# The first 34 microseconds of a hybrid decoder step: one norm chain per x tile, a new load order, no low half on GpSimd

## The chip, the cores and the metric

One core of a Trainium2 chip runs the whole program. The metric is the device time of one execution in microseconds; lower is better. The kernel before and after the change compute the same.

## The reference, cut to what matters

The kernel is one inference step of a decoder layer: 1024 prompt rows and 8 sample rows, width 1024. Everything begins with an RMS norm and one wide projection:

```
h = rms_norm(x, ln_g)              # y = x * rsqrt(mean(x*x) + 1e-6) * g, float32
proj = h @ w_in                    # w_in: 1024 x 3480, float32
q_raw, kv_raw, g_raw, z_nsa, u_rw, z_rw, q_mem, z_mem = split_in(proj)
```

The columns feed three groups of heads (sparse attention, an RWKV-7 recurrence, attention into a memory). The recurrence has its 896 columns `u_rw` (from column 1816) mixed with the row before: `u = u_cur + (prev - u_cur) * mu`. The groups are gated, concatenated, projected by `w_out` and added to x. Only the norm and the first 256 of the `u_rw` columns (two blocks of 128) lie in the code that is changed.

## The kernel before, in words

Matmuls keep float32 precision by splitting: each operand is a high part rounded to a shorter format plus a low part (the remainder), and a product is three matmuls: high weight by high h, high weight by low h, low weight by high h. In the profile they are `whi`, `wlo` and `h` (both parts).

The beginning stands in `phase1`. `warm` issues `WARM` matmuls of the identity by itself (tile `p_w`) while the first loads are under way. `load_xs` loads the 8 sample rows, squares them on ScalarE and scales them on VectorE. The SyncE queue loads, in this order: the first block of 128 weight columns (`w_load`, 512 KB, tile `wraw`), the four x tiles of the first half of the prompt (`load_x`, 128 rows and 512 KB each, tile `x`), the second weight block, the four x tiles of the second half. `w_split` makes a block's high half on ScalarE (`whi`, line 273) and its low half on VectorE (`wlo`, line 274), or on GpSimd, as for the second block here. The raw weights have two buffers, and so have the split ones; a third block's load waits until the first block is split, and its split waits until the first block's matmuls are done.

`square_x` squares x tiles on ScalarE with a row sum (`sqx`, line 186). `norm_x` takes two x tiles at a time: `rsqrt` is a chain of small VectorE operations (lines 126 to 137, tiles `rq_a`, `rq_g`, `rq_t`, `rq_r`; 12 of them for two columns, 9 for one column), and then the tiles are scaled in place, three on VectorE (line 197) and one on ScalarE (line 195).

`make_hT` transposes two x tiles (256 prompt rows, a "half" in what follows) on TensorE (tile `p_h`, line 223), eight slices of 128 columns; each slice is then taken out of PSUM as a high part on ScalarE (line 232) and a low part on VectorE (line 233). `make_hTs` does this for the sample rows; their last step, 16 small operations, is GpSimd's (lines 253 and 254), and they are the last 8 of the 520 columns of the tiles `h`. `u_half(0)` makes blocks 0 to 6 of `u_rw`. Blocks 0 and 1 are done in pieces as the halves come: block 0 columns 0 to 256, block 1 the same, then columns 256 to 520 of both. A piece is 24 matmuls (8 slices by 3). `do_u` takes a finished block out of PSUM. From block 2 on a block is 48 matmuls in one go.

The second half of the prompt (`xs1`) is squared after the last high part of the first, normed with the same functions, and transposed between blocks 2 to 6.

The order in which each engine gets its instructions is made at compile time by a list scheduler: it takes instructions in the order in which the code names them, but puts a later one first when the earlier is not ready by its own estimate of times. `tc.issue_after(ins)` ties the instructions of a block of code, on the engine of `ins`, behind it. From the end of this beginning on, TensorE's order is the order of the code (`InOrder`). In front of the engines' queues nothing is reordered: an instruction that waits holds up all that stand behind it on its engine.

Of the kernel before, what the change touches and what calls it, by code (L numbers as in the profile page):

```python
# [19 lines left out]
D = 1024  # L20
T = 1024
NS = 8
# [16 lines left out]
WARM = 34  # L39
# [75 lines left out]
class Step:  # L115
# [65 lines left out]
    def square_x(self, xs):  # L181
        nc = self.nc
        ss = self.small.tile([128, 2], F32, name="ss_x")
        for t, x in enumerate(xs):
            j = self.xp.tile([128, D], BF, name="sqx", tag="sqx", bufs=1)
            self.last_sq = nc.scalar.activation(j[:], x[:], AF.Square, accum_out=ss[:, t:t + 1])
        return ss

    def norm_x(self, xs, t0, ss=None):
        nc = self.nc  # L190
        ss = ss or self.square_x(xs)
        r = self.rsqrt(self.small, ss[:], 2, 1.0 / D, 1e-6)
        for t, x in enumerate(xs):
            if t and t0:
                nc.scalar.activation(x[:], x[:], AF.Copy, scale=r[:, t:t + 1])
            else:
                self.last_x = nc.vector.tensor_scalar(x[:], x[:], r[:, t:t + 1], None, op0=OP.mult)
            self.xn[t0 + t] = x
# [6 lines left out]
    def load_xs(self):  # L205
        nc, I = self.nc, self.I
        x = self.xsn = self.xp.tile([128, D], F32, name="xs", tag="xs")
        nc.scalar.dma_start(x[:NS], I["x_sample"][:, 0, :])
        ss = self.small.tile([128, 1], F32, name="ss_s")
        j = self.xp.tile([128, D], BF, name="sqx", tag="sqx", bufs=1)  # L210
        nc.scalar.activation(j[:NS], x[:NS], AF.Square, accum_out=ss[:NS])
        r = self.rsqrt(self.small, ss[:NS], 1, 1.0 / D, 1e-6, parts=NS)
        nc.vector.tensor_scalar(x[:NS], x[:NS], r, None, op0=OP.mult)

    def make_hT(self, H, half):

        nc = self.nc
        for k0 in range(0, 8, 2):
            pool, tag = (self.pw, "w") if k0 % 4 and H == 0 else (self.ptr, "tr")
            ps = pool.tile([128, 2, 256], F32, name="p_h", tag=tag)  # L220
            for j in range(2):
                for t in range(2):
                    nc.tensor.transpose(ps[:, j, t * 128:(t + 1) * 128],
                                        self.xn[2 * half + t][:, (k0 + j) * 128:(k0 + j + 1) * 128], self.ident[:])
            for j in range(2):
                k = k0 + j
                if len(self.hi[H]) <= k:
                    for x, y in zip((self.hi[H], self.lo[H]), (y[k] for y in self.h8) if H == 0 else self.h_tiles(H, k)):
                        x.append(y)
                g, c = self.v("ln_g", k), slice(half * 256, half * 256 + 256)  # L230
                hi, lo = self.hi[H][k], self.lo[H][k]
                self.last_hi = nc.scalar.activation(hi[:, c], ps[:, j], AF.Copy, scale=g)
                self.last_lo = nc.vector.scalar_tensor_tensor(lo[:, c], ps[:, j], g, hi[:, c].bitcast(F32),  # L233
                                                              op0=OP.mult, op1=OP.subtract)
                yield
# [193 lines left out]
    def phase1(self):  # L429
# [8 lines left out]
        with ExitStack() as ctx:  # L438
# [19 lines left out]
            with ExitStack() as xctx:  # L458
# [4 lines left out]
                self.load_xs()  # L463
                raws = [self.w_load(1816, 128)]
                xs0 = self.load_x(0, range(4))
                raws.append(self.w_load(1816 + 128, 128))
                xs1 = self.load_x(1, range(4))
                self.ready = [self.w_split(raws[0], 128)]
                self.norm_x(xs0[:2], 0)
                scaled = self.last_x.ins  # L470
                self.norm_x(xs0[2:], 2)
                self.ready.append(self.w_split(raws[1], 128, G))
                self.h8 = list(zip(*(self.h_tiles(0, k) for k in range(8))))
                with tc.issue_after(scaled):
                    self.make_hTs()
                first = self.u_half(0)
                with tc.issue_after(self.last_sq.ins):
                    for half in range(2):
                        for _ in self.make_hT(0, half):
                            pass  # L480
                        for _ in range(4):
                            next(first)
                with tc.issue_after(self.last_sq.ins):
                    self.rwkv_open()
                for _ in range(16):
                    next(first)
# [1886 lines left out]
```

## Time and profile before

| | |
|---|---|
| median of 3 runs | 1006.16 us (1002.08 to 1006.5) |
| profiled execution | 1003.45 us |
| its span, first to last instruction | 1001.1 us |
| mean granted TensorE clock | 0.991 |
| TensorE matmuls busy | 948.8 us, 95% |
| VectorE busy | 681.4 us, 68% |
| ScalarE busy | 446.8 us, 45% |
| GpSimd busy | 254.0 us, 25% |

Times in the profile count from the start of the span. PE is TensorE, PEld its loading of weights, DVE VectorE, ACT ScalarE, POOL GpSimd, SP SyncE; a q behind the name is the engine's queue of DMA issues. "L233" is line 233 of the kernel. In a timeline row stand start, length, engine, line, operation, output<-input, shapes and count, and in brackets how long the engine was idle before and what ended that. A row with a count above one merges neighbours. A matmul's length overlaps that of the next, so its rate is read from the starts.

### The profile page before, as it was taken

The numbers are of one execution on the slowest core, as the hardware profiler recorded it, in microseconds if no ns is written. First come the engines' busy times: TensorE is split into PE (matmuls) and PEld (weight loads), VectorE is DVE, ScalarE is ACT, GpSimd is POOL, SyncE is SP. The second block draws the span as 40 slices with busy tenths as digits, with TensorE's granted clock in tenths as the row PEclk, the third lists the DMA queues.
The fourth block names the chain that finished last, engine by engine and source line by source line (L and its number), as shares of the span: only waits on it lengthen the run. The fifth ranks groups of instructions, "written<-read, shape, count | busy, mean of one in ns | idle before, by whom it ended". The sixth has DMA issues, their size and how long they took to land.

```text
span 1001.1 us, 24786 instructions
## 1 busy us (share of the span) xinstructions
PE 948.8 (95%) x9955; PEld 788.9 (79%) x9955; DVE 681.4 (68%) x1954; ACT 446.8 (45%) x1005; POOL 254.0 (25%) x221
## 2 busy tenths in 40 slices
PE   7999999999999998999987999999999988998997
PEld 7998888878887887788865777887878876877874
DVE  6759589756684997633548677676869986357364
ACT  6754224223522432224436656665476665224212
POOL 2000000000000000000008776766578853112010
PEclk9999999999999999999999999999999999999999
DMA  8321313212321162265255223411200064984412
GB/s 283 95 75 40 90 34 117 76 45 74 85 77 34 49 178 67 61 158 135 81 159 171 86 81 116 149 43 45 59 22 16 28 149 130 324 276 160 158 65 76
DMA packets 133978, 104.20 MB, mean 104 GB/s; under 512 B 34593, under 2 KB 121128, under 8 KB 133736
## 3 DMA queue, kind: packets, MB, share of 16 engines
q1 hardware_dynamic: 128904, 90.92, 30.8%
q0 software_dynamic: 3200, 10.49, 3.0%
q8 instruction: 78, 1.28, 0.5%
q10 hardware_dynamic: 1760, 1.21, 0.4%
q14 instruction: 36, 0.29, 0.1%
HBM read 84.00 MB, written 22.78 MB: 107 GB/s over the span
## 4 chain that ended last, share of the span: by engine, by line
PE 65%; DVE 18%; ACT 6%; issue 4%; DMA 3%; POOL 2%; SPq 2%; ACTq 0%; DVEq 0%; POOLq 0%
PE p_pr L87 20%; PE p_pr L284 8%; PE p_out L87 5%; PE p_s L87 4%; PE p_pT L87 4%; PE p_o L87 3%; ACT p L1338 2%; POOL p L1352 2%; PE p_iy L87 2%; DVE nm L1337 1%; PE p_hid L87 1%; PE p_z L87 1%; PE p_it L87 1%; ACT p L1347 1%; DVE pt L1298 1%
## 5 line engine op out<-in xcount | busy, mean ns | idle before, releaser
L1352 POOL TENSOR_SCALAR p<-p,fac 128x640 f32<-128x640 f32 (+7 forms) x128 | 211.5, 1666 | 89.6 <-DVE fac L1349 34.6
L87 PE MATMUL p_pr<-h,whi 128*128 128x512 f32 (+5 forms) x928 | 231.0, 340 | 0.3 <-issue 0.3
L87 PEld LDWEIGHTS p_pr<-h,whi 128*128 128x128 f32 (+1 forms) x928 | 147.3, 184 | 19.0 <-issue 3.0
L87 PE MATMUL p_pr<-h,wlo 128*128 128x512 f32 (+5 forms) x464 | 152.5, 329 | 0.0
L999 POOL MEMSET w2d<- 128x128 f32 x1 | 0.2, 205 | 399.8 <-PE p_yy L87 399.8
L87 PEld LDWEIGHTS p_pr<-h,wlo 128*128 128x128 f32 (+1 forms) x464 | 85.1, 183 | 9.7
L284 PE MATMUL p_pr<-h,whi 128*128 128x256 f32 (+2 forms) x416 | 88.3, 308 | 0.4 <-DVE h L233 0.4
L87 PE MATMUL p_pT<-ident,p 128*128 128x128 f32 x528 | 72.8, 280 | 7.0 <-POOL p L1352 3.5
L87 PE MATMUL p_s<-kh,qs 128*128 128x512 f32 (+3 forms) x191 | 71.1, 380 | 1.9 <-ACT p L1338 1.8
L87 PEld LDWEIGHTS p_pT<-ident,p 128*128 128x128 f32 x528 | 56.8, 140 | 19.6 <-issue 7.1
L87 PE MATMUL p_o<-pt,vs 128*64 128x128 f32 x1056 | 70.0, 282 | 1.1 <-DVE c_r L1272 0.7
L1338 ACT ACTIVATE p<-p_s,nm 128x640 f32<-128x640 f32 (+3 forms) x64 | 55.7, 873 | 32.6 <-DVE nm L1337 26.2
L284 PEld LDWEIGHTS p_pr<-h,whi 128*128 128x128 f32 x416 | 67.4, 192 | 3.6 <-DVE h L233 0.6
L1337 DVE TENSOR_REDUCE nm<-p_s 128x1 f32<-128x640 f32 (+3 forms) x64 | 57.6, 918 | 14.9 <-PE p_s L87 14.9
L274 DVE TENSOR_TENSOR wlo<-wraw,whi 128x1024 fp32r<-128x1024 f32 (+1 forms) x34 | 40.7, 1197 | 35.2 <-ACT whi L273 35.1
L87 PEld LDWEIGHTS p_o<-pt,vs 128*64 128x64 f32 x1056 | 59.0, 140 | 6.7 <-issue 2.7
L284 PE MATMUL p_pr<-h,wlo 128*128 128x256 f32 (+2 forms) x208 | 63.3, 306 | 0.0
L87 PE MATMUL p_s<-kl,qs 128*128 128x512 f32 (+3 forms) x192 | 61.7, 338 | 0.0
L273 ACT ACTIVATE whi<-wraw 128x1024 fp32r<-128x1024 f32 (+1 forms) x35 | 36.4, 1039 | 50.9 <-PE p_pr L87 36.8
L1298 DVE COPY pt<-p_pT 128x512 f32<-128x512 f32 (+1 forms) x72 | 47.8, 670 | 16.2 <-PE p_pT L87 15.9
L1296 ACT ACTIVATE pt<-p_pT 128x512 f32<-128x512 f32 (+1 forms) x72 | 42.1, 587 | 27.6 <-PE p_pT L87 27.2
L87 PE MATMUL p_out<-woh,chi 128*128 128x512 f32 x128 | 52.5, 410 | 0.8 <-ACT woh L2194 0.6
(539 smaller groups left out, 2005.2 us busy)
## 6 DMA issues: line engine op xcount, KB each, us to landing
wraw<-in_w_in_dram SPq DMA_DIRECT2D x34, 512.0 KB
pg<-in_c_pool_dram SPq DMA_DIRECT2D x40, 256.0 KB
pg<-in_c_pool_dram SPq DMA_DIRECT2D x48, 128.0 KB
x<-in_x_prompt_dram SPq DMA_DIRECT2D x8, 512.0 KB
z_d<-zt SPq DMA_DIRECT2D x16, 256.0 KB
cat<-z_d SPq DMA_DIRECT2D x8, 512.0 KB
xres<-in_x_prompt_dram POOLq DMA_DIRECT2D x16, 256.0 KB, 3.8
wor<-in_w_out_dram SPq DMA_DIRECT2D x16, 256.0 KB
```

The lines of the kernel that those rows point to most:

```text
L87: self.last = getattr(self.engine, op)(*a, **k)
L273: nc.scalar.activation(hi[:, :, :n], raw[:, :, :n], AF.Copy)
L274: (low or nc.vector).tensor_tensor(lo[:, :, :n], raw[:, :, :n], hi[:, :, :n].bitcast(F32), op=OP.subtract)
L284: self.last_mm = self.pe.matmul(ps[:m, :b - a], w[:, k, :m], h[k][:, a:b], start=(k == 0 and i == 0), stop=(k == 7 and i == 2))
L999: nc.gpsimd.memset(w2d[:], 0.0)
L1296: nc.scalar.activation(pt[:, :n], ps[:, :n], AF.Copy)
L1298: nc.vector.tensor_copy(pt[:, :n], ps[:, :n])
L1337: V.tensor_reduce(nm[:, h, b:b + 1], ps[:, c0:n1], axis=AX.X, op=OP.max, negate=True)
L1338: A.activation(Ps[h, b][:, :n1 - c0], ps[:, c0:n1], AF.Exp, bias=nm[:, h, b:b + 1], accum_out=sm[:, h, b:b + 1])
L1347: A.activation(Ps[h, b][:, :n1], ps[:, h, :n1], AF.Exp, bias=nm[:, h, b:b + 1], accum_out=sm[:, h, b:b + 1])
L1352: nc.gpsimd.tensor_scalar(x, x, f[:, h, b:b + 1], None, op0=OP.mult)
```

## The change

Seven things change, all in the beginning:

- The warm-up is 24 matmuls instead of 34.
- x tiles 0 and 1 are loaded ahead of the first weight block, tiles 2 and 3 behind it.
- Every x tile has its own square, its own chain of nine operations and its own scaling; of the first four the last is scaled on ScalarE, of the second four every other one.
- Block 0 is split after x tile 1 is squared (ScalarE) and scaled (VectorE).
- Block 1's low half is made on VectorE, after block 0's first piece.
- The transposes of the first 256 rows go with block 0's first piece; those of the second 256 rows are tied behind the twelfth matmul of block 1's first piece. `make_hT` takes slices in the order 0, 4, 1, 5, 2, 6, 3, 7. In a piece of blocks 0 and 1 all matmuls with the low weights come last, 8 of 24.
- The sample rows' chain, scaling and transposes come later in the code.

```diff
-WARM = 34
+WARM = 24
...
-    def square_x(self, xs):
-        nc = self.nc
-        ss = self.small.tile([128, 2], F32, name="ss_x")
-        for t, x in enumerate(xs):
-            j = self.xp.tile([128, D], BF, name="sqx", tag="sqx", bufs=1)
-            self.last_sq = nc.scalar.activation(j[:], x[:], AF.Square, accum_out=ss[:, t:t + 1])
-        return ss
-
-    def norm_x(self, xs, t0, ss=None):
-        nc = self.nc
-        ss = ss or self.square_x(xs)
-        r = self.rsqrt(self.small, ss[:], 2, 1.0 / D, 1e-6)
...
+    def norm_x(self, x, t, engine):
+        nc = self.nc
+        ss = self.small.tile([128, 1], F32, name="ss_x")
+        j = self.xp.tile([128, D], BF, name="sqx", tag="sqx", bufs=1)
+        self.last_sq = nc.scalar.activation(j[:], x[:], AF.Square, accum_out=ss[:])
+        r = self.rsqrt(self.small, ss[:], 1, 1.0 / D, 1e-6)
+        if engine is nc.scalar:
+            self.last_x = nc.scalar.activation(x[:], x[:], AF.Copy, scale=r)
+        else:
+            self.last_x = nc.vector.tensor_scalar(x[:], x[:], r, None, op0=OP.mult)
+        self.xn[t] = x
...
+    def norm_xs(self):
+        x = self.xsn
+        r = self.rsqrt(self.small, self.ss_s[:NS], 1, 1.0 / D, 1e-6, parts=NS)
+        self.nc.vector.tensor_scalar(x[:NS], x[:NS], r, None, op0=OP.mult)
...
     def make_hT(self, H, half):
-        for k0 in range(0, 8, 2):
-            pool, tag = (self.pw, "w") if k0 % 4 and H == 0 else (self.ptr, "tr")
+        for k0 in range(4):
+            pool, tag = (self.pw, "w") if k0 % 2 and H == 0 else (self.ptr, "tr")
...
+                    k = k0 + 4 * j
...
                 raws = [self.w_load(1816, 128)]
-                xs0 = self.load_x(0, range(4))
+                xs0 += self.load_x(0, range(2, 4))
                 raws.append(self.w_load(1816 + 128, 128))
                 xs1 = self.load_x(1, range(4))
-                self.ready = [self.w_split(raws[0], 128)]
-                self.norm_x(xs0[:2], 0)
-                scaled = self.last_x.ins
-                self.norm_x(xs0[2:], 2)
-                self.ready.append(self.w_split(raws[1], 128, G))
+                for t in range(2):
+                    self.norm_x(xs0[t], t, nc.vector)
+                with tc.issue_after(self.last_sq.ins), tc.issue_after(self.last_x.ins):
+                    self.ready = [self.w_split(raws[0], 128)]
+                for t in range(2, 4):
+                    self.norm_x(xs0[t], t, nc.scalar if t == 3 else nc.vector)
                 self.h8 = list(zip(*(self.h_tiles(0, k) for k in range(8))))
-                with tc.issue_after(scaled):
-                    self.make_hTs()
                 first = self.u_half(0)
                 with tc.issue_after(self.last_sq.ins):
-                    for half in range(2):
-                        for _ in self.make_hT(0, half):
-                            pass
-                        for _ in range(4):
-                            next(first)
+                    for _ in self.make_hT(0, 0):
+                        pass
+                    next(first)
+                self.ready.append(self.w_split(raws[1], 128))
+                next(first)
+                self.norm_xs()
+                with tc.issue_after(self.last_mm.ins):
+                    for _ in self.make_hT(0, 1):
+                        pass
+                next(first)
+                self.make_hTs()
                 with tc.issue_after(self.last_sq.ins):
                     self.rwkv_open()
...
                 with tc.issue_after(self.last_hi.ins):
-                    sss = [self.square_x(xs1[t:t + 2]) for t in (0, 2)]
-                for t in (0, 2):
-                    self.norm_x(xs1[t:t + 2], t, sss[t // 2])
+                    for t in range(4):
+                        self.norm_x(xs1[t], t, nc.scalar if t % 2 else nc.vector)
...
     def u_half(self, H):
-        for pieces in ((0, 256),), ((256, 520),):
+        for a, b in (0, 256), (256, 520):
             for j, out in enumerate(begun):
-                hi, lo = self.ready[j]
-                for n, _ in enumerate(self.project(H, hi, lo, 128, out, pieces)):
-                    yield
-                if len(out) == 2:
+                ps = self.ppr.tile([128, 512], F32, name="p_pr", tag="pr")
+                parts = [(k, i) for k in range(8) for i in range(2)] + [(k, 2) for k in range(8)]
+                for n, (k, i) in enumerate(parts):
+                    if (a, j, n) == (0, 1, 12):
+                        yield
+                    hi, lo = self.ready[j]
+                    w, h = ((hi, self.hi[0]), (hi, self.lo[0]), (lo, self.hi[0]))[i]
+                    self.last_mm = self.pe.matmul(ps[:, :b - a], w[:, k, :], h[k][:, a:b], start=(n == 0), stop=(n == 23))
+                out.append((ps, a, b))
+                if a:
                     self.do_u(H, out, j)
+                yield
```

Ahead of the line `raws = [...]` of the new code stands `xs0 = self.load_x(0, range(2))`.

More of the change, by code (lines that the diff above doesn't have):

```diff
@@ L179, in load_x @@
         return xs
-    def square_x(self, xs):
+    def norm_x(self, x, t, engine):
         nc = self.nc
-        ss = self.small.tile([128, 2], F32, name="ss_x")
-        for t, x in enumerate(xs):
-            j = self.xp.tile([128, D], BF, name="sqx", tag="sqx", bufs=1)
-            self.last_sq = nc.scalar.activation(j[:], x[:], AF.Square, accum_out=ss[:, t:t + 1])
-        return ss
-    def norm_x(self, xs, t0, ss=None):
-        nc = self.nc
-        ss = ss or self.square_x(xs)
-        r = self.rsqrt(self.small, ss[:], 2, 1.0 / D, 1e-6)
[L193 to L198, printed above, removed]
+        ss = self.small.tile([128, 1], F32, name="ss_x")
[7 more added lines that the diff above has]
+        self.xn[t] = x
     def warm(self):
@@ L208, in load_xs @@
         nc.scalar.dma_start(x[:NS], I["x_sample"][:, 0, :])
-        ss = self.small.tile([128, 1], F32, name="ss_s")
+        self.ss_s = self.small.tile([128, 1], F32, name="ss_s")
         j = self.xp.tile([128, D], BF, name="sqx", tag="sqx", bufs=1)
-        nc.scalar.activation(j[:NS], x[:NS], AF.Square, accum_out=ss[:NS])
-        r = self.rsqrt(self.small, ss[:NS], 1, 1.0 / D, 1e-6, parts=NS)
-        nc.vector.tensor_scalar(x[:NS], x[:NS], r, None, op0=OP.mult)
+        nc.scalar.activation(j[:NS], x[:NS], AF.Square, accum_out=self.ss_s[:NS])
+    def norm_xs(self):
+        x = self.xsn
+        r = self.rsqrt(self.small, self.ss_s[:NS], 1, 1.0 / D, 1e-6, parts=NS)
+        self.nc.vector.tensor_scalar(x[:NS], x[:NS], r, None, op0=OP.mult)
     def make_hT(self, H, half):
         nc = self.nc
-        for k0 in range(0, 8, 2):
-            pool, tag = (self.pw, "w") if k0 % 4 and H == 0 else (self.ptr, "tr")
+        for k0 in range(4):
+            pool, tag = (self.pw, "w") if k0 % 2 and H == 0 else (self.ptr, "tr")
             ps = pool.tile([128, 2, 256], F32, name="p_h", tag=tag)
@@ L222, in make_hT @@
                 for t in range(2):
+                    k = k0 + 4 * j
                     nc.tensor.transpose(ps[:, j, t * 128:(t + 1) * 128],
-                                        self.xn[2 * half + t][:, (k0 + j) * 128:(k0 + j + 1) * 128], self.ident[:])
+                                        self.xn[2 * half + t][:, k * 128:(k + 1) * 128], self.ident[:])
             for j in range(2):
[L226 to L229, printed above, removed]
+                k = k0 + 4 * j
+                if len(self.hi[H]) < 8:
+                    for n, x in enumerate((self.hi[H], self.lo[H])):
+                        x += self.h8[n] if H == 0 else [None] * 8
+                if self.hi[H][k] is None:
+                    self.hi[H][k], self.lo[H][k] = self.h_tiles(H, k)
                 g, c = self.v("ln_g", k), slice(half * 256, half * 256 + 256)
@@ L463, in phase1 @@
                 self.load_xs()
+                xs0 = self.load_x(0, range(2))
                 raws = [self.w_load(1816, 128)]
-                xs0 = self.load_x(0, range(4))
+                xs0 += self.load_x(0, range(2, 4))
                 raws.append(self.w_load(1816 + 128, 128))
                 xs1 = self.load_x(1, range(4))
-                self.ready = [self.w_split(raws[0], 128)]
-                self.norm_x(xs0[:2], 0)
-                scaled = self.last_x.ins
-                self.norm_x(xs0[2:], 2)
@@ L483, in phase1 @@
+                self.norm_xs()
[4 more added lines that the diff above has]
+                self.make_hTs()
                 with tc.issue_after(self.last_sq.ins):
                     self.rwkv_open()
-                for _ in range(16):
-                    next(first)
+                next(first)
+                next(first)
                 self.xn = {}
                 with tc.issue_after(self.last_hi.ins):
-                    sss = [self.square_x(xs1[t:t + 2]) for t in (0, 2)]
```

## The prediction

> **What bounds the kernel now.** I read the page's headline and the chain that ended last first: is there one bound, and does time won in the first microseconds reach the end?
>
> ```profile
> span 1001.1 us, 24786 instructions
> PE 948.8 (95%) x9955; PEld 788.9 (79%) x9955; DVE 681.4 (68%) x1954; ACT 446.8 (45%) x1005; POOL 254.0 (25%) x221
> PE 65%; DVE 18%; ACT 6%; issue 4%; DMA 3%; POOL 2%; SPq 2%; ACTq 0%; DVEq 0%; POOLq 0%
> ```
>
> TensorE is busy for 95% of the span and is two thirds of the chain; DMA is 3%. So behind the beginning the program is one string of compute, and a start that comes X us earlier should end X us earlier, unless the order of the queues behind it changes. The change touches only what lies ahead of the third weight block. Next I read the chain in order of time, its stretch from 0 to 80 us (start, length, what):
>
> ```profile
> 1.70 5.76 DMA x<-in_x_prompt_dram
> ...
> 15.85 1.85 DVE rq_t L136
> ...
> 18.58 0.67 DVE x L197
> ...
> 19.30 0.73 PE p_h L223 x4
> ...
> 25.24 8.99 PE p_pr L284 x74
> ...
> 34.46 11.28 PE p_pr L284 x92
> ```
>
> The first x tile's landing, the norm chain on VectorE, the x scaling and transposes carry the time up to 19 us; from 25 us on it is matmuls. Then TensorE's waits and the windows between the moments where its clock changes (columns: PE, PEld, DVE, ACT, POOL busy with counts, granted clock, DMA share, GB/s):
>
> ```profile
> PE p_h L223 <- DVE x L197: 2.5, 1, 2.5
> PE p_pr L284 <- DVE h L233: 0.4, 1, 0.4
> 9.87:13.28 3.41, 3.39 (x34) 3.18 (x32) 2.95 (x14) 2.70 (x6) 0.00 (x0) 1.00 1.09 382
> 13.28:16.70 3.42, 2.94 (x22) 2.31 (x20) 3.15 (x14) 2.76 (x6) 2.65 (x10) 1.00 1.02 415
> 16.70:20.11 3.41, 0.91 (x8) 0.76 (x7) 3.41 (x8) 1.86 (x5) 2.60 (x8) 1.00 1.06 291
> 20.11:23.52 3.41, 3.41 (x19) 3.41 (x18) 2.06 (x5) 1.27 (x4) 0.00 (x0) 0.50 0.51 146
> ```
>
> TensorE stands 2.5 us for a scaled x tile, is busy 0.91 us in that window, and has a granted clock of 0.50 in the next: 3.41 us at half rate, 1.7 us lost. The timeline tells why the scaling was late, and gives the durations:
>
> ```profile
> 2.81 9.59 PE L203 MATMUL p_w<-ident 128*128 128x128 f32 x68 [2.81 <-DMA ident<-in_c_mat_dram]
> 4.37 0.14 DVE L126 TENSOR_SCALAR rq_a<-ss_s 8x1 f32<-8x1 f32 x1 [1.35 <-ACT sqx L211]
> 5.32 0.21 DVE L133 SCALAR_TENSOR_TENSOR rq_t<-rq_r,rq_a 8x1 f32<-8x1 f32 x1
> 6.21 1.06 ACT L273 ACTIVATE whi<-wraw 128x1024 fp32r<-128x1024 f32 x1 [1.87 <-DMA wraw<-in_w_in_dram]
> 7.29 1.23 DVE L274 TENSOR_TENSOR wlo<-wraw,whi 128x1024 fp32r<-128x1024 f32 x1 [1.77 <-ACT whi L273]
> 7.54 1.06 ACT L186 ACTIVATE sqx<-x 128x1024 bf16<-128x1024 f32 x1 [0.28 <-DMA x<-in_x_prompt_dram]
> 8.51 0.19 ACT L186 ACTIVATION_READ_ACCUMULATOR sqx<-x 128x1 f32 x1
> 9.95 0.17 DVE L126 TENSOR_SCALAR rq_a<-ss_x 128x2 f32<-128x2 f32 x1 [0.17 <-ACT sqx L186]
> 11.28 1.06 ACT L186 ACTIVATE sqx<-x 128x1024 bf16<-128x1024 f32 x1 [0.16 <-DMA x<-in_x_prompt_dram]
> 12.19 1.42 DVE L197 TENSOR_SCALAR x<-x,rq_r 128x1024 f32<-128x1024 f32 x2
> 12.33 0.66 PE L246 MATMUL p_hs<-ident,xs 8*128 8x8 f32 x8
> 13.00 2.30 PE L223 MATMUL p_h<-ident,x 128*128 128x128 f32 x16
> 15.34 2.34 POOL L274 TENSOR_TENSOR wlo<-wraw,whi 128x1024 fp32r<-128x1024 f32 x1
> 15.77 1.93 DVE L136 TENSOR_TENSOR rq_t<-rq_t,rq_a 128x2 f32<-128x2 f32 x1
> 18.28 1.15 ACT L195 ACTIVATE x<-x,rq_r 128x1024 f32<-128x1024 f32 x1 [1.55 <-DVE rq_r L137]
> 23.88 1.36 PE L223 MATMUL p_h<-ident,x 128*128 128x128 f32 x11
> 24.45 2.40 ACT L232 ACTIVATE h<-p_h,vec 128x256 fp32r<-128x256 f32 x6
> 24.99 2.46 DVE L233 SCALAR_TENSOR_TENSOR h<-p_h,vec,h 128x256 fp32r<-128x256 f32 x6
> 27.86 0.29 PE L284 MATMUL p_pr<-h,whi 128*128 128x264 f32 x1
> 33.16 1.22 DVE L274 TENSOR_TENSOR wlo<-wraw,whi 128x1024 fp32r<-128x1024 f32 x1
> 33.60 0.64 PE L284 MATMUL p_pr<-h,whi 128*128 128x256 f32 x4
> 34.44 0.38 PE L284 MATMUL p_pr<-h,wlo 128*128 128x256 f32 x1
> ```
>
> While GpSimd makes block 1's low half (15.34 to 17.68), one two-column VectorE operation takes 1.93 us where its kin take about 0.17; it ends with GpSimd's. It sits in the norm chain of x tiles 2 and 3, whose scaling TensorE awaits. At 33.60 block 2 begins, and from there TensorE runs on: 33.60 is my measuring point.
>
> **The change part by part.** First TensorE's work up to that point, which stays. Matmuls follow each other every 0.12 us (27.86 to 33.60 is 48 of them): blocks 0 and 1 are four pieces of 24, each 2.9, in all 11.5. A transpose takes 0.11 (the 11 in a row, less the last one's tail): 16 for a half are 1.75. The eight of the samples take 0.66. In all 15.7; before, 12.33 to 33.60 is 21.3, so 5.6 us are lost, of which 2.5 and 1.7 are named above. That is the ceiling, plus what the earlier first tile gives.
>
> *Loads.* Tile x0 takes block 0's place as first big transfer. Block 0 was awaited until 6.21, x0 until 7.54. The first place cannot be worse than 6.2; x tiles are then 1.25 us apart (7.54 to 11.28 is three), so x0 between 4.9 (one step less) and 6.2: I take 5.5, x1 6.8, block 0 8.7. The fifth transfer still ends at 11.3, so x3 is no earlier, and the split of block 0 moves back to 8.7 to 9.8 on ScalarE, where nothing waits for it yet. Block 2's load now waits for a split that ends some 4 us later; it stands behind the second half's four x tiles anyway, costs nothing, and lands far ahead of its use at 30.
>
> *Norm chains.* A chain for one tile is 9 operations, 0.19 apart (five steps from 4.37 to 5.32): 1.8 us with its end, against 2.2 for the chain of two (9.95 to 12.19). Four chains instead of two are 7.2 against 4.4: 2.8 more on VectorE, and as much again for the second half's tiles. But x0's can start when its square is read, 5.5 + 1.06 + 0.19 = 6.7. VectorE then: chain 0 to 8.5, scaling of 0.7 to 9.2, chain 1 to 11.0, scaling to 11.7. The samples' chain (2.5 with scaling) loses its rank, but has its input at 4.34 and finds VectorE idle; I cost it at nothing. If it came after x1 it would cost 2.5 there.
>
> *First transposes*: 11.7 against 13.0, done at 13.5. The warm-up (68 pieces for 34 matmuls) loses 20 pieces, at 0.10 (34 in the window from 9.87) to 0.14 each (the mean of the 9.59 us): it ends at 9.6 to 10.4, and a hole of some 1.7 us follows. In front of the transposes nothing needs TensorE, so only the clock can make this cost (rival d).
>
> *Low half of block 1*: 2.34 us of GpSimd go, and with them 1.93 - 0.17 = 1.8 of VectorE's stall; 1.2 of VectorE come instead (the row at 7.29). Its matmuls come last in the new order of a piece, so it is not awaited until some 22 us.
>
> *Half 0 of block 0.* From 11.7 VectorE owes block 0's low half (1.2, to 12.9), chain 2, scaling, chain 3 (4.3) and eight low tiles of h, 0.41 each. The first seven are needed before the fourth of eight slices can be multiplied, since tiles are made in the order 0, 4, 1, 5, 2, 6, 3 and used in the order 0 to 7. The seventh is there at 15.8 with no chain between, at 20.1 behind both chains. In the trace such chains and low tiles interleave; I take 17.5. Then 17 matmuls: 19.5.
>
> *The rest*: 12 matmuls of block 1 to 20.9, sixteen transposes to 22.65, 12 matmuls to 24.05. x3, scaled on ScalarE (1.15, and what stands behind it on that queue, the tiles of h among it, waits with it, as at 18.28 before) after chain 3, is there at about 21. The second half's tiles of h cost 0.40 each on ScalarE and 0.41 on VectorE from 21.3 on, the seventh at about 24.6, needed at 24.05 + 0.7: hidden, by a hair; if the other 2 us of VectorE work fall there, they show. The samples' transposes (0.66) may fill a hole before 17; if not, they come here. Two pieces of 2.9 end at 29.9, or 30.5. The fourth piece takes over the first one's PSUM slot as before, once U has been read from it, and rwkv_open's loads stay behind the last square on ScalarE's queue: no term for either.
>
> *Block 2's low half* is late by nearly nothing now (33.16 + 1.22 = 34.38, its matmul starts at 34.44 and two transposes filled the gap). With 2.8 us more of chains on VectorE around it, it costs 0 to 1.5; I take 0.2.
>
> Sum: 33.6 to 30.1, that is 3.5 us. Ends: everything hidden, 15.7 us straight from 11.7 gives 27.4, a gain of 6.2; low tiles behind both chains, the samples late and 1.5 for block 2 give 33.7 and no gain. Against the profiled execution, 1003.45 us (its span 1001.1 and 2.35 around it), that is 999.95; that execution is 2.7 under the median of the three runs, 1006.16, which would go to 1002.7.
>
> **The rivals.**
> (a) *Nearly all comes*: chains and low tiles overlap well, VectorE keeps up, 5 to 6 us: 1000.6. For it: the 5.6 us lost are all waits or half clock. Against: VectorE is the scarcest engine there, 3.15 and 3.41 of 3.4 us in two windows, and gets more to do.
> (b) *The place of the GpSimd stall is taken by VectorE's own queue*: low tiles behind chains 2 and 3. Seventh at 20.1, block 0's half done at 22.1, block 2 at 32.7 to 33.3: a gain of 0.5, time 1005.7. For it: in the old timeline most low tiles stand behind the chain.
> The third rests on GpSimd's part in the samples' columns:
>
> ```profile
> 14.01 1.12 POOL L253 CAST h<-hs 128x8 fp32r<-128x8 f32 x8 [11.94 <-DVE hs L249]
> 17.65 1.65 POOL L254 TENSOR_TENSOR h<-hs,h 128x8 fp32r<-128x8 f32 x7
> ```
>
> (c) *Slower*: as (b), and with TensorE idling in pieces from 14 to 20 the clock goes to half for one more window (1.7 us at a time when it is the bound) and the samples' columns come late: GpSimd makes these after TensorE's and VectorE's parts, and the second pieces of blocks 0 and 1 read them. Sixteen operations are 2.8 to 3 us, against 2 us of matmuls that consume them: 1 to 1.6 us. Then 33.3 + 1.7 + 1.6 = 36.6, slower by 3: 1009.2. It decides from the point where the samples' tile reaches GpSimd later than 22 us.
>
> (d) *A colder start*, for the clock: the window 16.70 to 20.11 with 0.91 of 3.41 busy was followed by a clock of 0.50, the one with 2.94 was not. The new hole of 1.6 us leaves its window about half busy, between these two. If it drops, a matmul takes twice 0.12 for one window; a slice's two then take 0.48, little more than a low tile (0.41) lets them, so it hides but for some 0.5 us: 1003.2. I give it 0.25 within the main case, without a time of its own. The Trainium skill, TensorE: Matmul & The Clock Gate, Part 4, has a harsher rule: transposes do not count as work for the clock gate. By that rule nothing counts from 10 us to the first matmul at about 13.5, a whole window, and the drop is sure; were it not hidden at all, the time would be the main one plus 1.7, 1004.4. No window of this trace holds transposes alone, so the rule is open here.
>
> **How the numbers follow.** Main case 0.50, 1002.7, its own range 1000.5 to 1004.5; (a) 0.25; (b) 0.15; (c) 0.10. Changes of queue order far behind the beginning, and the spread of the three runs (1002.08 to 1006.5), add about 2 us to each side. Range: 998.5 from (a) less 2, to 1007.0, which takes in (b) and half of (c). About 0.5%, 5 us, is what a measurement of this kernel can tell from no change; most of the gain that I forecast is below it. Faster by more than that is (a) and the better part of the main case's luck: 0.30. Slower is a part of (c): 0.05. Same: 0.65.
>
> **What would show it.** Block 2's first matmul at about 30; no VectorE operation of two columns or one over 0.3 us; first transposes at about 11.7; no wait of 2.5 us of the transposes for x; block 0's first piece ending near 19.5, with many small waits for h; clock of 1.00 from 20 us on. Wrong, if block 2 starts after 32 (queue order, or samples late: see the GpSimd rows), or if it starts at 30 and the time does not follow, in which case the order behind it changed.

## The result

Ten runs of each kernel: before 1004.46 us (1001.75 to 1009.14), after 1013.22 us (1008.6 to 1014.51). Time ratio after to before 1.0085, 95% interval [1.0066, 1.0104]: slower by 0.85%, where 1002.7 us was forecast. The profiled run of after took 1014.47 us.

**The profile after.** The headline, TensorE's busy row and the shares of the chain that ended last:

```profile
span 1012.7 us, 24775 instructions
PE 954.4 (94%) x9935; PEld 793.0 (78%) x9935; DVE 682.3 (67%) x1978; ACT 448.4 (44%) x1006; POOL 251.8 (25%) x220
PE 62%; DVE 19%; ACT 7%; DMA 5%; issue 3%; SPq 2%; POOL 1%; ACTq 0%; POOLq 0%; DVEq 0%
```

TensorE's share of the chain fell from 65% to 62%. TensorE's timeline of the beginning (start, length, what; in brackets the idle time before and its releaser):

```profile
10.28 0.60 PE L220 MATMUL p_h<-ident,x 128*128 128x128 f32 x4
11.88 1.53 PE L220 MATMUL p_h<-ident,x 128*128 128x128 f32 x12 [0.99 <-DVE x L190]
...
15.83 1.33 PE L578 MATMUL p_pr<-h,whi 128*128 128x256 f32 x9 [1.10 <-ACT whi L272]
...
19.82 1.12 PE L578 MATMUL p_pr<-h,wlo 128*128 128x256 f32 x8
...
22.35 1.09 PE L578 MATMUL p_pr<-h,wlo 128*128 128x256 f32 x8
23.94 0.63 PE L245 MATMUL p_hs<-ident,xs 8*128 8x8 f32 x8 [0.49 <-DVE h L232]
25.41 0.39 PE L578 MATMUL p_pr<-h,whi 128*128 128x264 f32 x1 [0.84 <-POOL h L252]
26.25 0.39 PE L578 MATMUL p_pr<-h,whi 128*128 128x264 f32 x1 [0.45 <-DVE ulast L319]
29.50 0.66 PE L220 MATMUL p_h<-ident,x 128*128 128x128 f32 x2 [2.86 <-DVE rq_t L133]
31.82 1.54 PE L220 MATMUL p_h<-ident,x 128*128 128x128 f32 x6 [1.66 <-ACT x L188]
33.01 3.65 PE L578 MATMUL p_pr<-h,whi 128*128 128x264 f32 x15
...
40.79 0.40 PE L283 MATMUL p_pr<-h,whi 128*128 128x256 f32 x2
```

The first pieces of blocks 0 and 1 are done at 23.44 (22.35 + 1.09); the forecast had 24.05. Two second pieces of 24 matmuls remained, 5.8 us, yet block 2 starts at 40.79, not at 30 (before: 33.60). The 17.35 us between are 5.8 of matmuls, 0.63 for the samples' transposes, 0.9 for eight transposes at the forecast's 0.11, and the five bracketed waits from 23.94 on: 0.49 + 0.84 + 0.45 + 2.86 + 1.66 = 6.3. Some 3.7 are left; the windows between clock changes tell where they went (PE, PEld, DVE, ACT, POOL busy, granted clock, DMA share, GB/s):

```profile
23.95:27.36 3.41, 1.40 (x10) 0.90 (x10) 3.29 (x15) 2.78 (x7) 2.15 (x15) 1.00 0.00 0
27.36:30.77 3.41, 0.66 (x2) 0.29 (x2) 3.24 (x22) 3.33 (x8) 0.25 (x2) 0.51 0.00 0
30.77:34.19 3.42, 2.37 (x11) 2.37 (x12) 2.96 (x16) 2.19 (x3) 0.00 (x0) 0.50 0.08 22
34.19:37.60 3.41, 3.41 (x18) 3.41 (x17) 0.88 (x2) 2.07 (x4) 0.00 (x0) 0.50 0.00 0
37.60:41.00 3.40, 3.40 (x29) 3.40 (x29) 2.28 (x6) 1.97 (x5) 0.00 (x0) 0.99 0.17 24
```

Three windows run at half clock, with TensorE busy for 6.4 us in them; half of that, 3.2 us, is lost. The other 0.5 us stay open.

What TensorE waits for at 29.50 and 31.82 is not needed by the matmuls of blocks 0 and 1 at all: it is x tiles 4 and 5, of the second half, which none of blocks 0 to 6 reads. Their eight transposes stand in TensorE's queue behind the first matmul of each second piece, and ahead of the other 46. In the compiled program (output<-input; cut):

```
p_pr_442<-h00_0,whi_199 128x264
p_pr_476<-h00_0,whi_315 128x264
p_h_634<-ident,x_157   (x tiles 4 and 5, eight transposes up to here)
...
p_pr_442<-h10_0,whi_199 128x264
```

VectorE's, ScalarE's and GpSimd's rows of the same stretch:

```profile
19.37 0.13 DVE L126 TENSOR_SCALAR rq_a<-ss_s 8x1 f32<-8x1 f32 x1
21.16 0.74 DVE L209 TENSOR_SCALAR xs<-xs,rq_r 8x1024 f32<-8x1024 f32 x1
24.89 0.21 DVE L248 TENSOR_TENSOR hs<-p_hs,vec 128x64 f32<-128x64 f32 x1
28.61 0.75 DVE L190 TENSOR_SCALAR x<-x,rq_r 128x1024 f32<-128x1024 f32 x1
...
25.38 1.05 ACT L185 ACTIVATE sqx<-x 128x1024 bf16<-128x1024 f32 x1
30.62 1.15 ACT L188 ACTIVATE x<-x,rq_r 128x1024 f32<-128x1024 f32 x1
...
25.17 1.08 POOL L252 CAST h<-hs 128x8 fp32r<-128x8 f32 x8 [23.10 <-DVE hs L248]
```

The samples' chain, whose input is there before 5 us, begins at 19.37 and GpSimd gets its tile at 25.17. The second half's first square starts at 25.38, x4 is scaled at 28.61 and x5 on ScalarE at 30.62, behind the squares of x6 and x7.

**Beyond the beginning.** Block 2 starts 7.2 us later; the spans of the two profiles differ by 11.6, the medians by 8.8. In the compiled program the order of TensorE's matmuls is the same in both kernels from about the 500th of some 7,300 on. What differs there is the clock. One stretch as an example, before and then after:

```profile
515.00:550.00 35.00, 26.13 (x176) 18.17 (x174) 28.38 (x81) 19.69 (x47) 23.09 (x12) 0.95 0.62 192
```

```profile
515.00:550.00 35.00, 26.65 (x117) 18.36 (x116) 22.07 (x71) 15.90 (x35) 14.72 (x8) 0.85 0.67 199
```

TensorE is busy for some 75% there, and 0.95 against 0.85 is 3.5 against 10.5 us of half clock. Such windows come and go between runs of one kernel: of 100 runs of the kernel before, taken beside the experiments, those with a mean clock of up to 0.986 have a median of 1006.6 us, those from 0.991 up 1002.0. So 7.2 us are put down to the change itself, and the remaining 1.6 of the medians to later clock windows; no run separates the two.

### The profile page after: what moved, and what is told of

It is laid out like the page before. It is cut to its first block, busy times and chain, and to the rows that moved or that the text cites. A ratio compares the mean times of both kernels' runs of the same rounds, so it can differ in the third digit from the quotient of the medians.

```text
span 1012.7 us, 24775 instructions
## 1 busy us (share of the span) xinstructions
PE 954.4 (94%) x9935; PEld 793.0 (78%) x9935; DVE 682.3 (67%) x1978; ACT 448.4 (44%) x1006; POOL 251.8 (25%) x220
## 4 chain that ended last, share of the span: by engine, by line
PE 62%; DVE 19%; ACT 7%; DMA 5%; issue 3%; SPq 2%; POOL 1%; ACTq 0%; POOLq 0%; DVEq 0%
PE p_pr L87 18%; PE p_pr L283 6%; PE p_out L87 5%; PE p_s L87 5%; PE p_pT L87 4%; PE p_o L87 4%; ACT p L1349 2%; PE p_iy L87 2%; DMA wor<-in_w_out_dram 1%; ACT p L1358 1%; PE p_hid L87 1%; PE p_z L87 1%; DVE nm L1348 1%; PE p_it L87 1%; PE p_sc L87 1%
## 5 line engine op out<-in xcount | busy, mean ns | idle before, releaser
L283 PE MATMUL p_pr<-h,whi 128*128 128x256 f32 (+2 forms) x352 | 74.1, 307 | 0.3 <-ACT whi L272 0.3
L283 PEld LDWEIGHTS p_pr<-h,whi 128*128 128x128 f32 x352 | 56.1, 189 | 3.3 <-ACT whi L272 0.8
L283 PE MATMUL p_pr<-h,wlo 128*128 128x256 f32 (+2 forms) x176 | 53.7, 306 | 0.0
```

The costliest lines, as they stand in the source:

```text
L283: self.last_mm = self.pe.matmul(ps[:m, :b - a], w[:, k, :m], h[k][:, a:b], start=(k == 0 and i == 0), stop=(k == 7 and i == 2))
```

## The experiments

Theory at first: TensorE's queue (transposes of the second half ahead of the second pieces) and the late samples. Rivals: one-tile chains on VectorE, the new order of pieces, the shorter warm-up. The start of block 2 is from the one profiled run of each kernel, with the half-clock windows that fell into it; the ratio is to the kernel before on the same chip. The experiments ran on three chips, so times of different rows are best compared by their ratios.

| kernel | block 2 at | median us | ratio and interval |
|---|---|---|---|
| before | 33.60 | 1004.46 | 1 |
| after | 40.79 | 1013.22 | 1.0085 [1.0066, 1.0104] |
| e1 after, weave tied | 38.05 | 1012.7 | 1.0082 [1.0058, 1.0106] |
| e2 after, samples first | 38.18 | 1010.15 | 1.0063 [1.0042, 1.0084] |
| e3 both of these | 38.27 | 1013.05 | 1.0077 [1.005, 1.0104] |
| e4 before, low half on VectorE | 29.49 | 1001.56 | 0.9964 [0.9944, 0.9984] |
| e5 after, queues mended | 35.42 | 1007.39 | 1.0039 [1.0016, 1.0063] |
| e6 after, samples behind x1 | 35.09 | 1011.15 | 1.0087 [1.0068, 1.0107] |
| e7 e6, block 2's split first | 35.78 | 1008.91 | 1.0047 [1.0022, 1.0073] |
| e8 after, second half's chains in pairs | 40.04 | 1014.0 | 1.0111 [1.0089, 1.0132] |
| e9 e5, warm-up 34 | 34.35 | 1012.03 | 1.008 [1.0059, 1.0102] |
| e10 e5, samples early | 31.55 | 1005.93 | 1.0027 [1.0007, 1.0048] |
| e11 e10, warm-up 34 | 32.52 | 1005.73 | 1.001 [0.9989, 1.003] |
| e12 e4, x tiles 0 and 1 first | 30.71 | 1003.85 | 1.0001 [0.998, 1.0021] |
| e13 e11, first half's chains in pairs | 31.65 | 1005.63 | 1.0002 [0.9983, 1.0021] |
| e14 e12, one-tile chains in the first half | 30.83 | 1005.4 | 0.9993 [0.9976, 1.001] |
| e15 e4, warm-up 24 | 30.32 | 1003.06 | 0.9976 [0.9955, 0.9997] |

**e1: tie the second half's transposes behind the last matmul of block 1's second piece.** (`weave` sets these transposes between the matmuls of blocks 2 to 6.)

```
+ with tc.issue_after(self.last_mm.ins):
      for _ in weave(group(first, 8), chain(self.make_hT(1, 0), self.make_hT(1, 1))):
          pass
```

> The changed kernel, with the transposes of the second half of the prompt and blocks 2 to 6 tied behind the last matmul of block 1; nothing else. Theory Q (queue order: in the changed kernel eight of these transposes stand in TensorE's queue ahead of 46 of the 48 matmuls of the second pieces, and wait 2.9 and 1.7 us for x tiles 4 and 5; the idle time then costs clock): the two waits and the half clock go, block 2 starts at 31 to 32 instead of 40.8, time 1002 to 1004, that is 8 to 11 us under the changed kernel. Rival S (the samples' columns come late from GpSimd and hold up both second pieces): block 2 still starts after 36, time above 1009. Rival V (four chains of one tile instead of two of two crowd VectorE): block 2 starts after 36 as well, since x tiles 4 to 7 are as late as before and block 2's low half too.

The tie worked for TensorE: the second pieces ended near 35. But block 2 began at 38.05 only, with a new wait (TensorE's, then ScalarE's timeline) and, behind it, 1.4 us for the low half:

```profile
PE p_pr L283 <- ACT whi L272: 2.9, 1, 2.9
```

```profile
35.09 1.15 ACT L188 ACTIVATE x<-x,rq_r 128x1024 f32<-128x1024 f32 x1 [1.69 <-DVE rq_r L137]
...
36.94 1.06 ACT L272 ACTIVATE whi<-wraw 128x1024 fp32r<-128x1024 f32 x1 [0.71 <-DMA gains<-in_nsa_k_norm_dram]
```

Block 2's high half stands on ScalarE behind the scaling of x7, which itself waits 1.69 us for VectorE. The same blockage, one engine further on. Block 2 was expected at 31 to 32.

**e2 and e3: the samples' chain ahead of x0's and their transposes ahead of block 0** (`self.norm_xs()` behind `xs1 = self.load_x(...)`, `self.make_hTs()` ahead of `first = self.u_half(0)`), without and with e1's tie.

> The changed kernel, with the samples' norm chain ahead of x tile 0's in the code and their transposes ahead of block 0; no tie. Theory Q: the second pieces no longer wait for GpSimd, but transposes of the second half still stand in the queue ahead of block 2, and x tile 5 is scaled at about 31; TensorE waits 2 to 3 us there and may lose clock: block 2 at 33 to 36, time 1004 to 1008. Rival S: with the samples early everything is mended, block 2 at 30, time 1001.

> Both edits: samples early, and the second half's transposes tied behind block 1. Theory Q: block 2 at 29 to 30.5, 1 to 2 us less than with the tie alone, time 1000 to 1002.5. Rival V: VectorE's queue still bounds, no gain over the tie alone.

Both start block 2 at about 38.2. In e2 VectorE's queue blocks instead: the samples' product waits for transposes that stand behind the warm-up, and x0's chain behind it.

```profile
11.19 0.23 DVE L248 TENSOR_TENSOR hs<-p_hs,vec 128x64 f32<-128x64 f32 x1 [2.89 <-PE p_hs L245]
12.24 0.74 DVE L190 TENSOR_SCALAR x<-x,rq_r 128x1024 f32<-128x1024 f32 x1
```

x0 is scaled at 12.24, 3.8 us later than the 8.41 of the kernel after. So neither run tells what the samples are worth when placed well.

**e4: of the whole change only the low half, in the kernel before.**

```
- self.ready.append(self.w_split(raws[1], 128, G))
+ self.ready.append(self.w_split(raws[1], 128))
```

> The kernel before, with one part of the change alone: block 1's low half on VectorE instead of GpSimd. My step: a stall of 1.8 us of VectorE goes and 1.2 us of work come, the wait of 2.5 us for the scaled x tile shrinks, and with it the window at half clock (1.7 us) goes: block 2 at 31 to 32.5 instead of 33.6, time 1 to 2.5 us under the kernel before. Rival: VectorE is full there, what it no longer waits it now works: block 2 at 33 to 34, no change.

Faster than both kernels: 0.9964 [0.9944, 0.9984]. Block 2's first matmul, and the window of the old stall:

```profile
29.49 0.64 PE L284 MATMUL p_pr<-h,whi 128*128 128x256 f32 x4
```

```profile
14.80:18.20 3.40, 2.86 (x21) 2.39 (x20) 3.40 (x15) 2.23 (x6) 2.25 (x14) 1.00 1.07 384
```

Block 2 comes 4.1 us earlier: both losses that the prediction named in the old profile (2.5 of waiting, 1.7 of half clock) go at once.

**e5: the kernel after with three queue places mended:** block 2's split is issued ahead of the second half's norm, the half's ScalarE scalings behind that split, the weave behind a second-piece matmul.

```
+ tied = self.last_mm.ins
+ with tc.issue_after(tied):
+     next(first)
  self.xn = {}
  ...
+ with tc.issue_after(tied):
      for _ in weave(group(first, 8), chain(self.make_hT(1, 0), self.make_hT(1, 1))):
```

> The changed kernel with the samples as late as in it, but with both queues put right by hand: block 2's split and its first matmuls stand in the code ahead of the second half's norm, the second half's scalings on ScalarE are tied behind block 2's high half, its transposes behind block 1. With the tie alone the second pieces ended at 35.0, and then block 2 waited 2.9 us for its high half, which stood on ScalarE behind the scaling of x tile 7 and six loads, and 1.4 us for its low half. Theory Q2 (what holds TensorE is the second half's norm work, which stands ahead of block 2's on one queue or another): block 2 at 35 to 36, no wait of over 1 us in front of it, 3 to 4.5 us under the tie alone in the profile, time about 1008.5 to 1010. Rival V (four chains crowd VectorE): block 2's low half comes late all the same, block 2 waits 2 us or more, time as with the tie alone.

Block 2 at 35.42, 5.4 us ahead of after; 1007.39 us. What was left: samples still late (second pieces from 28.06), and two half-clock windows, the first of them here, under the row with the longest hole in front of it:

```profile
16.12 1.32 PE L585 MATMUL p_pr<-h,whi 128*128 128x256 f32 x9 [1.10 <-ACT whi L272]
...
14.39:17.80 3.41, 2.00 (x13) 1.55 (x13) 3.41 (x18) 2.30 (x6) 0.00 (x0) 1.00 1.03 399
17.80:21.21 3.41, 3.41 (x17) 3.41 (x18) 3.17 (x12) 1.48 (x2) 0.00 (x0) 0.50 0.98 248
```

The profiled run of after has no half-clock window there, though the code up to there is the same. In e5 the first pieces end at 25.26, in after at 23.44. Counted from there, block 2 comes after 10.16 us in e5 and after 17.35 in after, so the mended places are worth 7.2 us, of which e5's earlier window hides 1.8.

**e6 and e7: the samples tied behind x1's scaling and their transposes put ahead of block 0; e7 with block 2's split first as well.**

> The changed kernel with one thing undone: the samples' chain and transposes stand in the code where they did before, tied on VectorE behind the scaling of x tile 1 (so that, unlike in the run with the samples in front of everything, they can't hold up tile 0's chain), and ahead of block 0. No tie of the transposes. Theory L (the samples' place is the root: because they are late, the second pieces are planned late, and the second half's work is put in front of them): the two waits of the transposes and the wait for GpSimd go without any tie, block 2 at 30 to 31.5, time 1001 to 1003.5, 9 to 12 us under the changed kernel. Rival V: block 2 after 34, time 1007 or more.

> The kernel with the samples behind x tile 1, and with block 2's split and first matmuls ahead of the second half's norm in the code, the transposes tied behind block 1. Theory L: the queues are right already with the samples early, so this adds 0 to 1 us: block 2 at 30 to 31, time 1000.5 to 1002.5. Theory Q2: adds more, 1 to 2 us.

Both miss their forecasts. TensorE has the samples' transposes in the midst of x1's and stands for them:

```profile
17.64 1.02 PE L245 MATMUL p_hs<-ident,xs 8*128 8x8 f32 x8 [5.27 <-DVE xs L209]
```

That is e6 (6.2 us in e7): a chain tied behind x1 is late there, as VectorE's order interleaves it with that of x2 and with low tiles.

But e6 answers where the second half's place in the queues comes from. Nothing ties its transposes there, and only the samples were moved; yet the transposes now stand behind the last matmul of the second pieces:

```profile
33.94 1.13 PE L581 MATMUL p_pr<-h,wlo 128*128 128x264 f32 x8
34.91 0.38 PE L220 MATMUL p_h<-ident,x 128*128 128x128 f32 x2
35.09 0.75 PE L283 MATMUL p_pr<-h,whi 128*128 128x256 f32 x4
```

In e2, where the samples were moved too, they stand there as well (from 34.89). So it is the late samples that put the second half's transposes ahead of the second pieces in the kernel after. That the scheduler does so because it plans the second pieces as not ready is argued, not shown. And e7, which adds two of e5's three mends to e6, gains little: from the end of the first pieces to block 2 it takes 5.84 us, e6 6.01 (and e6 then 0.99 of waiting for block 2's low half).

**e8: the kernel after, the second half's norm in pairs as before.**

> The changed kernel with the second half's norm as before the change: two chains of 12 operations for two tiles each, one scaling in four on ScalarE, squares ahead. Rival V (the chain per tile in the second half costs the time): block 2 at 33 to 35, time 1005 or less. Theory L: the samples are as late, the order of the queues stays (eight transposes of the second half ahead of the second pieces), so block 2 stays after 38, time 1010 to 1014.

Block 2 at 40.04, 1014.0 us. The transposes stand ahead of the second pieces as in after, and TensorE waits 4.3 us for one of their x tiles. The number of small VectorE operations in the second half is not the cause.

**e9 to e12: the 2 by 2 of samples and warm-up on e5's queues, and e4 with the new loads.** The edits: `WARM = 34` (e9, e11); the samples' chain traced ahead of x0's, their transposes ahead of block 0, with their product on VectorE tied behind x1's scaling (e10, e11); x tiles 0 and 1 loaded ahead of block 0 and their pair's norm traced ahead of its split (e12).

> The change with the queues mended (block 2's split and the half's transposes as in the run of that kind before, 1007.39 us, block 2 at 35.42) and the warm-up of 34 matmuls instead of 24. Theory W (the half-clock window at 17.8 comes from the shorter warm-up: TensorE ran 2.1 us of the 3.41 us before it): the window at 13 to 20 us is gone, first transposes move from 10.5 to about 12.7, block 2 comes at 33.5 to 34 (the window cost about 1.7) and the time is about 1005.5. Theory S (the window comes from the holes that the order of the first pieces leaves between 13 and 20 us, one of 1.10 for whi and one of 0.23 for h, and those stay): a window at 15 to 20 remains, block 2 at 35 to 36, time 1007 to 1008. Either way the second window, at 28, stays, as the samples' transposes are still late.

> The change with the queues mended, the samples' chain ahead of x0's and the samples' transposes ahead of block 0's matmuls, warm-up still 24. If the late samples cost what the trace of the mended version shows (TensorE at 25.2 with the first pieces done, second pieces from 28.06, of which 0.6 is the transposes themselves, and a half-clock window at 28 behind the hole): block 2 at about 31.5 to 32.5, no window at 28, time about 1004 to 1005; a window at 14 to 18 may remain (warm-up 24). Rival: the samples' chain ahead of x0's delays x0 by 1.9 us as in the run with the samples first, and that is passed on to the end: block 2 at 34 or later, time 1007 or more.

> As the one with the samples early, and a warm-up of 34. If queues, samples and warm-up are all that stood between the change and its forecast: no half-clock window before 36 us, block 2 at 29.5 to 30.5, that is 3 to 4 us ahead of the kernel before, and a time of about 1001 to 1002, as the version with the low half on VectorE alone (1001.56, block 2 at 29.49); the earlier x tiles then bring nothing beyond it, as the warm-up ends at 12.7. Rival (the first pieces are held by VectorE's low tiles and chains, whatever the queues): block 2 at 32 or later, time about 1004 or more, with waits for h and wlo of over 2 us on TensorE before 24 us.

> The kernel before with block 1's low half on VectorE (0.9964 alone, block 2 at 29.49) and x tiles 0 and 1 loaded ahead of block 0 with their pair's norm traced first; pairs, order of pieces, samples and warm-up of 34 as before. If the earlier x tiles are worth something by themselves: block 2 at 28 to 29, time about 1000.5 to 1001. Rival (TensorE's warm-up ends at 12.7 and the second pair of x tiles, which now lands later by block 0's weights in front of it, sets the end): block 2 at 29.5 to 30.5, time 1001.5 to 1002.5. Worse than 1003 would say that loading x first holds up block 0's weights, hence whi and wlo.

e10: block 2 at 31.55 against e5's 35.42, so with the warm-up of 24 the late samples cost 3.9 us; neither of e5's two half-clock windows comes. With the warm-up of 34 the same step, e9 to e11, is worth 1.8 (34.35 to 32.52). Counted from the end of the first pieces it wins 3.8 to 3.9 both times; but in e11, where the samples' transposes stand behind the longer warm-up, the first pieces end 2.1 us later than in e9 (26.12 against 24.06). e11: 1005.73; the forecast's gain is not reached even so. In e9 no half-clock window comes at 13 to 20 us; the one after the late samples stays (at 27):

```profile
13.40:16.80 3.40, 2.16 (x15) 1.57 (x14) 3.04 (x17) 3.20 (x8) 0.00 (x0) 1.00 1.03 417
16.80:20.20 3.40, 3.23 (x27) 3.03 (x27) 3.37 (x11) 2.00 (x3) 0.00 (x0) 1.00 1.05 307
```

yet its time, 1012.03, is far above e5's: what was won in the beginning was lost later. In the stretch shown above for before (0.95) and after (0.85) its clock is 0.71, against 0.80 in e5:

```profile
515.00:550.00 35.00, 27.29 (x113) 19.66 (x112) 23.60 (x79) 15.80 (x36) 19.31 (x10) 0.71 0.61 189
```

That stretch alone doesn't explain it: e10's clock there is 0.76, and its profiled run took 1003.87 us.

e12 was to show what earlier x tiles bring by themselves: block 2 at 30.71, 1.2 later than e4 and later than either forecast. ScalarE's timeline shows a cause:

```profile
8.56 1.06 ACT L273 ACTIVATE whi<-wraw 128x1024 fp32r<-128x1024 f32 x1 [1.99 <-DMA wraw<-in_w_in_dram]
9.52 1.04 ACT L186 ACTIVATE sqx<-x 128x1024 bf16<-128x1024 f32 x1
```

The square of x1 stands behind block 0's split, which now waits for the later load. So the pair's chain starts at 10.79 instead of 9.45, and the first transposes of x at 13.83 instead of 13.24; the other 0.6 us are lost behind that.

**e13 and e14: chains against order of pieces.** A square with e11 (new order, one-tile chains: 32.52) and e12 (old order, pairs: 30.71).

> The version with queues mended, samples early and a warm-up of 34 (block 2 at 32.52, 1005.73 us), but with the first half's norm in pairs as in the kernel before. If the one-tile chains cost the 2 us (24 small VectorE instructions instead of 12 between the low tiles): block 2 at 30.5 to 31, time about 1003.5 to 1004. If the order of pieces and transposes costs them: block 2 stays at 32 to 33, time 1005 to 1006.

> The kernel before with the low half on VectorE and x tiles 0 and 1 first (block 2 at 30.71, 1003.85 us), but with one-tile chains in the first half. If the chains cost the 2 us: block 2 at 32 to 33, time about 1005.5. If the order of pieces does: block 2 stays at 30 to 31, or a little earlier since x0 is scaled sooner (29.5), time 1003 to 1004.

e13 31.65, e14 30.83. The new order costs 0.9 (pairs) to 1.7 us (one-tile), the one-tile chains 0.1 (old order) to 0.9 (new). Differences of this size are of one profile each. In e11 TensorE waits for a low tile, all eight of which it now wants before the matmuls with block 0's low weights:

```profile
19.47 2.19 PE L587 MATMUL p_pr<-h,whi 128*128 128x256 f32 x15 [0.98 <-DVE h L232]
```

But e14, in the old order, waits 1.0 us for low tiles too. What in the new order costs the time is not shown. The step also takes in the other slice order and the places of the splits.

**e15: e4 with the shorter warm-up.**

> The kernel before with the low half on VectorE (block 2 at 29.49, 1001.56 us) and a warm-up of 24. TensorE's first other work stands at 12.66 there because x tiles and samples come late; with the warm-up ending near 10.3 a hole of about 2 us opens before it. If the hole tips a 3.4 us window to half clock (the theory that the warm-up's length keeps the clock up): a window somewhere in 13 to 20 us, block 2 at 31 to 31.5, time about 1003 to 1003.5. If not: block 2 at 29.5, time 1001 to 1002.

Block 2 at 30.32, 0.8 later, 1003.06 us; the half-clock window came, right behind the hole:

```profile
12.88 3.56 PE L223 MATMUL p_h<-ident,x 128*128 128x128 f32 x16 [2.29 <-DVE x L197]
...
9.40:12.80 3.40, 1.19 (x14) 0.98 (x12) 2.91 (x15) 2.70 (x6) 0.00 (x0) 0.99 1.08 369
12.81:16.22 3.41, 3.33 (x17) 3.17 (x17) 3.34 (x13) 2.24 (x4) 2.28 (x10) 0.51 1.03 418
16.22:19.63 3.41, 3.17 (x24) 2.77 (x23) 2.97 (x13) 2.17 (x7) 1.12 (x7) 1.00 1.04 300
```

On e5's queues and with the samples early the longer warm-up lost 1.0 (e10 to e11), as the transposes then wait for its end; with the samples late it gained 1.1 (e5 to e9). It is worth about one us either way.

## Why the prediction was wrong

The start of block 2 can be followed from before to after along the runs, one step each:

| step | runs | block 2 |
|---|---|---|
| low half on VectorE | before to e4 | 33.60 to 29.49: -4.1 |
| x tiles 0 and 1 first | e4 to e12 | to 30.71: +1.2 |
| new order of pieces, one-tile chains | e12 to e11 | to 32.52: +1.8 |
| warm-up 24 | e11 to e10 | to 31.55: -1.0 |
| samples late | e10 to e5 | to 35.42: +3.9 |
| second half's places in the queues | e5 to after | to 40.79: +5.4 |

A step's size depends on what is taken before it (the samples' is 1.8 with the warm-up of 34), and each is the difference of two single profiles.

*"Norm chains", the second half.* This step failed, and its price is the largest. The prediction counted the second half's chains as VectorE time (0 to 1.5 for block 2's low half) and never placed what they release: eight transposes in TensorE's queue ahead of 46 matmuls, the scalings in ScalarE's ahead of block 2's split. TensorE takes its queue in order, so it waited 2.86 and 1.66 us for tiles that none of blocks 0 to 6 reads. Three half-clock windows follow the holes. With those places mended 5.4 us are back. The number of chains didn't make these places: e8, with the old pairs, keeps them, and e2 and e6, with the samples moved ahead and nothing else, don't have them. So they hang on the next step.

*"The samples' chain … I cost it at nothing."* This step failed too. Its input being there, and VectorE being idle at 4.34, was taken as the time of execution. But the chain is traced behind x0 to x3 and shares the buffers of their chains (two of each kind), and the queue keeps it behind them: 19.37. Rival (c) had the mechanism and its mark, "the samples' tile reaches GpSimd later than 22 us": it came at 25.17. It was priced at 1 to 1.6; the timeline shows 1.97 us from 23.44 to 25.41, and the experiments 3.9 (warm-up 24) and 1.8 (warm-up 34). The rival's whole sum, block 2 at 36.6, still lacks what the late samples do to the second half's place in the queues; 40.79 was measured.

*"Low half of block 1"* was right, and too small: 1.8 us was VectorE's stall only, while the two losses that hang on it, named earlier in the prediction, are 4.2, and e4 measured 4.1. A sum against one ceiling hid that this one part by itself brings more than the 3.5 us forecast for all seven.

*"Loads" and "First transposes"* were right in their times (forecast 11.7; x0's four ran at 10.28, the other twelve at 11.88) and wrong in worth: e12 and e14, which have the earlier x tiles, start block 2 later than e4.

*"Half 0 of block 0" and "The rest"* held in their sum: first pieces done at 23.44, forecast 24.05. Their split didn't: block 0's first piece ended at 20.94, not 19.5, because matmuls of block 1 went ahead of its last ones. So what the forecast missed lies behind the first pieces, which it closed with "Two pieces of 2.9 end at 29.9, or 30.5".

*Rival (d), the clock.* In the profiled run of after its window didn't come: the clock is 1.00 up to 27.4. In e5, with the same code up to there, one came later, at 17.80, behind a wait of 1.10 us for a high half. A shorter warm-up alone does tip a window (e15: 1.19 of 3.40 us busy, then 0.51), and in that kernel it hid but for 0.8, near the 0.5 given. The rule in the Trainium skill (TensorE: Matmul & The Clock Gate, Part 4), that transposes do not engage the clock, isn't borne out: in e15 the window 12.81 to 16.22 holds nothing but x's transposes and one matmul begun at 16.20, and the next has a clock of 1.00.

*The range* ended at 1007.0, with 2 us for "changes of queue order far behind". The order behind the beginning did not change; the later clock windows did, between runs of one kernel too. Its base was high as well: 1006.16 was a median of three runs, and ten gave 1004.46. Against the start of block 2 the median times of the seventeen kernels lie 971 to 978 us later. Why e9 has the largest of these, 977.7, is open: no run sets the phase of the clock's windows, and none was tried.

The last paragraph of the prediction named the sign: "if block 2 starts after 32 (queue order, or samples late: see the GpSimd rows)". Both happened.

## What to carry to other kernels

When a change moves a producer, follow what it releases into every queue where that stands: an instruction that isn't ready blocks all behind it on its engine, however idle its input engine is. Test the parts alone before the whole: here one line (the low half on VectorE, 0.9964) carried the gain, and the other parts gave it back; e4 is the version to keep. A hole in TensorE can cost twice, once as a wait and again as a window at half clock behind it.

## What the hardware showed

The granted clock changes at the edges of windows of 3.41 us. How busy TensorE was in one window decides the next only roughly. In the runs above, 2.00 us busy were followed by 0.50 (e5) and 2.16 by 1.00 (e9), which looks like a limit; these two pairs of windows, from e5 and from e6, show that it isn't one:

```profile
519.53:522.94 3.41, 1.60 (x8) 0.87 (x6) 0.00 (x0) 1.20 (x3) 0.93 (x2) 1.00 0.94 322
522.94:526.36 3.42, 1.48 (x6) 0.91 (x7) 3.02 (x4) 1.78 (x3) 0.48 (x1) 1.00 0.63 149
```

```profile
704.97:708.38 3.41, 2.76 (x23) 2.38 (x23) 2.67 (x9) 1.60 (x4) 3.10 (x2) 1.00 0.73 180
708.38:711.79 3.41, 3.03 (x30) 2.63 (x28) 2.48 (x14) 1.31 (x5) 0.61 (x1) 0.50 0.02 4
```

1.60 us busy kept the clock, 2.76 lost it. Of some 4,700 such pairs from full clock, all that the seventeen profiles hold from 20 us on, every window under 1.47 us lost it and none over 2.77 did; between these the profile's busy time does not tell. The lowest that kept it, 1.47, is in e8, from 998.56. The Trainium skill (TensorE: Matmul & The Clock Gate, Why this matters for your kernels) warns of idle gaps above about 3 us; in e5's window from 14.39 no hole was longer than 1.10 us, and the clock fell all the same.
